# Two recurrences written step by step beside each other, their late inputs in DRAM, the last projection by halves, and a planner that knows matmul tilings

## The chip, the cores and the metric

One NeuronCore of a Trainium2 chip runs one program. Its engines run side by side and wait for each other through semaphores: TensorE (PE; its weight loads are listed as PEld), VectorE (DVE), ScalarE (ACT), GpSimd (POOL) and SyncE (SP), which issues all transfers of this kernel. Matmul operands lie in SBUF, matmul results go to PSUM, weights and spilled tensors lie in DRAM. The metric is device microseconds (us) of one execution, the median of three runs for the kernel before.

## The reference

512 tokens of 1024 columns pass through two blocks. The first has two layers: a gated feed-forward, a mixer (an mLSTM in the first layer, dilated attention in the second, each with cross-attention to 256 memory tokens), another feed-forward. The second block has two layers with a modulated input, and it also carries a context of 256 tokens. Each of its layers joins three mixers: grouped attention, neighbourhood attention, and a recurrence (RWKV-7) of 6 heads that runs over the tokens once forward and once backward:

```python
def _rwkv7_step(S, inp):
    r, w, k, v, kk, b = inp
    sa = jnp.einsum('bhvk,bhk->bhv', S, kk)
    S = S * w[:, :, None, :] - sa[..., None] * b[:, :, None, :] + v[..., None] * k[:, :, None, :]
    return S, jnp.einsum('bhvk,bhk->bhv', S, r)
...
    y_l = jnp.concatenate([yr_l * jax.nn.silu(rg_l), ya_l * jax.nn.silu(ag_l),
                           yn_l * jax.nn.silu(ng_l)], axis=-1) @ w_out
    x = _layer_norm(DEEPNORM_ALPHA * x + gate[:, None] * y_l, ln_g, ln_b)
```

The outputs of both directions are added, normalised by head and gated; then they are projected with the two attentions' outputs, added to x and layer-normalised. The context runs through the same recurrence first, and its final states start those of the tokens. In the second layer the context's outputs are not needed, only its states.

## The kernel before, in words

**Program and order.** The program does not issue instructions. It records operations on named tiles, with `par` weaving parallel branches together. `schedule` then orders the whole list: `simulate` is a list scheduler that runs once from the end (its finishing times become keys of urgency) and once from the start, three rounds. For each engine it takes the most urgent operation that can start, and SBUF and PSUM tiles are slots of a fixed number (`SLOTS`, line 265): 70 slots `t` of 2 KB per partition, 8 PSUM banks `ps`, 14 `S`, one `uv`. `Op._cost` gives durations and `LATENCY` the hops between engines. On TensorE it prefers, within `STAY` (2.0 us of the keys), an operation with the same flag `small` (planned cost under 0.1 us) as the last one. The order of the program's own text decides only among equals.

**Stages.** In order of time: the first layer's feed-forward with the context's input work; the mLSTM; the second feed-forward with the context's first recurrence (`ctx_out(0)`); shared keys and values; the same for the second layer of the first block, whose last feed-forward runs beside `ctx_out(1)`; then for each of the second block's layers `layer_in` (projections), `layer_mix` (attention woven with `rwkv`), `out2` (output projection and layer norm). Large projections are three float32r matmuls for each product (`mm3`), the attention's and the recurrence's products are float32, which the trace shows as two matmul instructions each.

**The recurrence.** Tokens are cut into chunks of 32, four to a block of 128. For one direction `r`, `rwkv_a` makes decays and transformed keys from `k`, `kk`, `r` of `rwkv_in`, and the masks' products `EB`, `EQ`; `rwkv_b` inverts triangular 32x32 systems with 62 small VectorE operations; `rwkv_c` turns the one tile `UV` (values, and under them the right-hand sides) into the recurrence's inputs; `rwkv_d` steps from chunk to chunk. A step has 6 products `pw` (weights from `S`, tiling 64x32), a subtraction on two halves of `UV` (DVE), 6 products `pn` (from `UV`, 64x64), and S = pn + keep (DVE), with keep = S times the decay on POOL. After four steps the block's outputs `y` are 24 products with the old states (64x32) and 12 with `UV` (128x64), written as four of the one and two of the other in turn. `rwkv` runs a, b, c, d for the forward direction and then for the backward one; both use the same `UV`, so the backward `rwkv_c` overwrites what the forward `rwkv_d` reads. The first direction writes `y` by ACT, the second adds to it on DVE. 512 tokens have 16 steps and 4 blocks in each direction, the context's 256 have 8 and 2.

**The last projection.** `out2` works on tokens 256 to 511 and then 0 to 255 (`cuts`). The attention's outputs, the residual and the split operands are loaded or made for all 512 tokens; `rwkv_y`, 192 matmuls of 256 columns, and the layer norm are done by halves. The backward direction, the last one, finishes blocks 3 and 2 first.

Of the kernel before, what the change touches and what calls it, by code (L numbers as in the profile page):

```python
# [16 lines left out]
P = 128  # L17
# [336 lines left out]
class Op:  # L354
    def __init__(self, eng, method, a, k):
        self.eng, self.method, self.a, self.k = eng, method, a, k
        named = [(f"#{i}", x) for i, x in enumerate(a)] + list(k.items())
        refs = [(q in ("#0", "out", "accum_out"), x) for q, x in named if isinstance(x, Ref)]
        self.writes = [x for w, x in refs if w]
        self.reads = [x for w, x in refs if not w]  # L360
        self.cost = self._cost()
        self.small = self.cost < 0.1 and eng == "tensor"

    def _cost(self):
# [3 lines left out]
        if self.eng == "tensor":  # L368
            n = self.writes[0].cols()
            if self.method == "transpose":  # L370
                return 0.84e-3 * n
# [69 lines left out]
def simulate(ops, before, after, key, lag, ahead):  # L441
# [12 lines left out]
    small = False  # L454
# [18 lines left out]
    def best(tight):  # L473
        out = None
        for e in ENGINES:
# [4 lines left out]
            for src, time in ((can[e], lambda x: free[e]), (wait[e], lambda x: x[0])):  # L480
                pick = None
                for x in sorted(src):
# [5 lines left out]
                    if pick and ops[i].small != small:  # L488
                        continue
                    at = room(i, tight)  # L490
                    if at is not None:
                        pick = (max(at, time(x)), key[i], i, e, src, x)
                        if e != "tensor" or src is not can[e] or ops[i].small == small:
                            break
# [6 lines left out]
    while len(order) < n:  # L501
# [6 lines left out]
        if e == "tensor":  # L508
            small = ops[i].small
# [19 lines left out]
def schedule(ops):  # L529
# [11 lines left out]
    lag = lambda i, j: 0.0 if ops[i].eng == ops[j].eng == "tensor" else LATENCY[ops[i].eng]  # L541
# [30 lines left out]
class Prog:  # L572
# [1055 lines left out]
    def rwkv_in(self, l, hp, n, need_y, cut=False):  # L1628
# [22 lines left out]
        d["kk"] = kk  # L1651
        d["v"] = [conv(6 + j) for j in range(3)]
        if need_y:
            d["vd"] = [self.save(v, (P, n)) for v in d["v"]]
            d["r"] = [conv(j) for j in range(3)]

        d["UV"] = self.new("uv", (P, nb, 2, 6, 64))
        for o in (0, 64):
            nc.gpsimd.memset(d["UV"][o:o + 32], 0.0)
        for j in range(3):  # L1660
# [3 lines left out]
            for par in range(2):  # L1664
                for c in range(4):
                    o = 64 * (c % 2 ^ par) + 32
                    self.act(d["UV"][o:o + 32, :, c // 2, 2 * j + par], pv[32 * c:32 * c + 32, :, 64 * par:64 * par + 64])
        return d

    def rwkv_a(self, l, d, r):  # L1670
# [4 lines left out]
        q = dict(D=self.sm((P, n // 32, 3)), KR=[], EB=[], EQ=[], kt=[], be=[])  # L1675
# [11 lines left out]
        if need_y:  # L1687
            first = "kd" not in d
            d.setdefault("kd", []), d.setdefault("pr", [])
        for j in range(3):  # L1690
            ps = self.ps((P, n))
# [12 lines left out]
            q["KR"].append(KR)  # L1704
            for hf in range(nh):
                sl = slice(256 * hf, 256 * hf + 256)
                kap, kc, ec = ch(KR[hf][:, 0]), ch(d["kk"][j][:, sl]), ch(eL[:, sl])
# [6 lines left out]
                if need_y:  # L1714
                    self.mul(KR[hf][:, 1], d["r"][j][:, sl], eL[:, sl])
# [6 lines left out]
            self.mul(bb, bb, d["kk"][j])  # L1722
            self.act(th, th, AF.Identity, scale=L["hka"][:, j:j + 1], bias=L["oka"][:, j:j + 1])
            self.mul(th, th, d["k"][j])
            if need_y and first:
                d["kd"].append(self.save(th, (P, n)))
            elif need_y:
                t = self.load(self.t2((P, n)), d["kd"][j])
                self.tt(t, t, th, ALU.add)
                self.stt(t, d["r"][j], self.c(f"r_k{l}", j), t, ALU.mult, ALU.mult)  # L1730
# [17 lines left out]
            for par in range(2):  # L1748
# [5 lines left out]
                for w, mask, out in [(0, strict, "EB"), (1, incl, "EQ")][:nk]:  # L1754
# [3 lines left out]
                    q[out].append(e.rearrange("p g c t -> p g (c t)"))  # L1758
# [44 lines left out]
    def rwkv_c(self, d, q):  # L1803

        n, nb = d["n"], d["nb"]
        q["zk"] = []
        for j in range(3):
            pb = [self.ps((P, nb, 64)) for _ in range(2)]
            for b in range(nb):
                for par in range(2):  # L1810
                    for a in range(2):
                        self.mm(pb[par][64 * a:64 * a + 64, b], q["EB"][2 * j + par][:, 2 * b + a], d["UV"][:, b, a, 2 * j + par])
# [4 lines left out]
            for par in range(2):  # L1817
# [8 lines left out]
                for c in range(4):  # L1826
                    ro = 64 * (c % 2 ^ par)
                    self.act(d["UV"][ro:ro + 32, :, c // 2, h], pu[32 * c:32 * c + 32, :, par], scale=-1.0)
# [3 lines left out]

    def rwkv_d(self, d, q, r, S):


        n, nb, need_y = d["n"], d["nb"], d["need_y"]
        UV = d["UV"]
        first = "y" not in d
        if first and need_y:
            d["y"] = [self.t2((P, 6, 64)) for _ in range(nb)]  # L1840
        both = [(j, par) for j in range(3) for par in range(2)]
        for step in range(4 * nb):
            g = 4 * nb - 1 - step if r else step
            b, c = g // 4, g % 4
            row = lambda c, par: 64 * (c % 2 ^ par)
            if step % 4 == 0:
                old = {}
                ps = self.ps((P, 2, 3, 64))
                pw, pn = ps[:, 0], ps[:, 1]
            old[c] = S  # L1850
            for j, par in both:
                o, ro = 64 * par, row(c, par)
                self.mm(pw[ro:ro + 32, j], q["zk"][j][o:o + 64, 32 * g:32 * g + 32], S[o:o + 64, j])
            keep = self.new("S", (P, 3, 64))
            self.nc.gpsimd.tensor_tensor(out=keep, in0=S, in1=q["D"][:, g].unsqueeze(2).to_broadcast([P, 3, 64]), op=ALU.mult)
            for par in range(2):
                ro = row(c, par)
                u = UV[ro:ro + 32, b, c // 2, par::2]
                self.tt(u, u, pw[ro:ro + 32], ALU.subtract)
            for j, par in both:  # L1860
                o, ro = 64 * par, row(c, par)
                self.mm(pn[o:o + 64, j], q["be"][j][g // 8][ro:ro + 64, g // 2 % 4, o:o + 64],
                        UV[ro:ro + 64, b, c // 2, 2 * j + par])
            S = self.new("S", (P, 3, 64))
            self.tt(S, pn, keep, ALU.add)
            if not need_y or step % 4 < 3:
                continue
            py = [self.ps((P, 3, 64)) for _ in range(2)]
            for a in range(2):
                for j in range(3):  # L1870
                    for i, par in ((0, 0), (0, 1), (1, 0), (1, 1)):
                        o, cc = 64 * par, 2 * a + (i ^ par)
                        s = P * (b % 2) + 32 * cc
                        self.mm(py[par][32 * cc:32 * cc + 32, j], q["KR"][j][b // 2][o:o + 64, 1, s:s + 32],
                                old[cc][o:o + 64, j], stop=False)
                    for par in range(2):
                        self.mm(py[par][64 * a:64 * a + 64, j], q["EQ"][2 * j + par][:, 2 * b + a], UV[:, b, a, 2 * j + par],
                                start=False)
            for par in range(2):
                y = d["y"][b][:, par::2]  # L1880
                if first:
                    self.act(y, py[par])
                else:
                    self.tt(y, y, py[par], ALU.add)
# [35 lines left out]
    def rwkv(self, l, d, S):  # L1920
        out = []
        for r in range(2):
            q = self.rwkv_a(l, d, r)
            self.rwkv_b(q, r)
            self.rwkv_c(d, q)
            if S is None:
                s0 = self.new("S", (P, 3, 64))
                self.nc.vector.memset(s0, 0.0)
            else:
                s0 = S[r]  # L1930
            out.append(self.rwkv_d(d, q, r, s0))
        return out

    def out2(self, l, d, gates, pa, src, dst, mod, w, n, nxt=None):
# [3 lines left out]
        h, lo = self.parts(n)  # L1938
        for k in range(3, KD):
# [149 lines left out]
```

## Time and profile before

| | |
|---|---|
| median of three runs | 3327.55 us (3325.96 to 3327.77) |
| profiled execution | 3327.22 us, of which the span from first to last instruction is 3325.4 us |
| TensorE | 3217.1 us busy, 21142 matmuls |
| VectorE, ScalarE, GpSimd | 2299.8, 1613.3, 252.0 us busy |
| TensorE clock granted, mean | 0.987 of full speed |
| transfers | 348.41 MB, 105 GB/s |

Busy time of an engine is the union of its instructions' times, and a matmul's end is modelled, so neighbouring matmuls overlap in the profile. What a matmul costs the engine is better read from start to start. All operations are recorded by one helper line, 568, so rows are told apart by tile names and shapes: `ps<-S,t 64*32 64x64` is a matmul into PSUM with weights from an `S` tile, 64 rows by 32 columns of the array, 64 columns streamed.

### The profile page before, as it was taken

Reading aid. Unit: us, or ns where it says so; the run is one execution under the profiler, and the core shown is the slowest. Engines: PE = TensorE matmul, PEld = TensorE weight load, DVE = VectorE, ACT = ScalarE, POOL = GpSimd, SP = SyncE. Lnnn points to the kernel's source line nnn. Section 1 sums busy time; section 2 is a strip of 40 time slices with the busy share of each in tenths; the row PEclk is TensorE's granted clock in tenths of the full one; section 3 lists DMA queues with packets and bytes.
Section 4 is the critical chain, followed back from the end, with each engine's and each line's share of the span. In section 5 each row is a group of like instructions: output and inputs, shape, how many; then the busy total and the mean of one; then the engine's idle time right before and its main releaser. Section 6 shows DMA issues by size and latency. Waiting matters only on the chain. (4 is left out here: it accounts for less than half of the span.)

```text
span 3325.4 us, 55255 instructions
## 1 busy us (share of the span) xinstructions
PE 3217.1 (97%) x21142; PEld 2604.3 (78%) x21142; DVE 2299.8 (69%) x4801; ACT 1613.3 (49%) x3579; POOL 252.0 (8%) x233
## 2 busy tenths in 40 slices
PE   8999999999999999999999999999999898999898
PEld 6788878778877788878886888777877678877677
DVE  9954686575669677677568657587475887575876
ACT  4433464363434344333338535344454974654773
POOL 0000000000000102000001000000120011111111
PEclk9999999999999999999999999999999999999899
DMA  6633332133213334344431422233222232322231
GB/s 227 205 114 124 120 116 80 56 117 101 82 55 101 108 117 143 114 137 154 130 103 38 133 88 89 69 102 120 89 83 93 66 118 94 107 87 85 63 121 43
DMA packets 153489, 348.41 MB, mean 105 GB/s; under 512 B 16644, under 2 KB 60420, under 8 KB 153224
## 3 DMA queue, kind: packets, MB, share of 16 engines
q1 hardware_dynamic: 153224, 344.87, 31.9%
q8 instruction: 166, 2.72, 0.3%
q14 instruction: 99, 0.81, 0.1%
HBM read 315.05 MB, written 29.76 MB: 104 GB/s over the span
## 5 line engine op out<-in xcount | busy, mean ns | idle before, releaser
L568 PE MATMUL ps<-t,t 128*128 128x512 f32 (+6 forms) x15204 | 2865.1, 351 | 63.7 <-DVE t L568 29.6
L568 PEld LDWEIGHTS ps<-t,t 128*128 128x128 f32 (+2 forms) x15204 | 2287.6, 182 | 522.6 <-issue 65.2
L568 ACT ACTIVATE t<-raw 128x512 fp32r<-128x512 f32 (+1 forms) x962 | 565.8, 612 | 762.5 <-PE ps L568 510.5
L568 DVE TENSOR_TENSOR t<-raw,t 128x512 fp32r<-128x512 f32 (+2 forms) x962 | 625.5, 670 | 235.3 <-PE ps L568 169.0
L568 ACT ACTIVATE t<-t 128x512 f32<-128x512 f32 (+8 forms) x739 | 377.7, 525 | 426.4 <-DVE t L568 246.2
L568 DVE TENSOR_TENSOR t<-t,t 128x256 f32<-128x256 f32 (+7 forms) x812 | 417.7, 544 | 91.3 <-ACT t L568 57.1
L568 ACT ACTIVATE t<-ps 128x512 f32<-128x512 f32 (+8 forms) x448 | 216.0, 511 | 219.5 <-PE ps L568 214.6
L568 DVE TENSOR_TENSOR t<-ps,t 128x512 f32<-128x512 f32 (+3 forms) x274 | 178.8, 657 | 185.3 <-PE ps L568 178.2
L568 POOL TENSOR_TENSOR s<-s,const 128x4 f32<-128x4 f32 (+6 forms) x65 | 110.2, 1698 | 1722.4 <-DVE s L568 1714.0
L568 PE MATMUL ps<-const,t 128*128 128x128 f32 (+1 forms) x1116 | 189.0, 291 | 22.5 <-ACT t L568 12.3
L568 DVE SCALAR_TENSOR_TENSOR t<-ps,t 128x512 f32<-128x512 f32 (+3 forms) x229 | 147.5, 648 | 69.2 <-PE ps L568 68.5
L568 PEld LDWEIGHTS ps<-const,t 128*128 128x128 f32 x1116 | 137.4, 149 | 66.1 <-ACT t L568 27.8
L568 PE MATMUL ps<-uv,t 64*64 64x64 f32 (+1 forms) x2208 | 144.1, 230 | 3.2 <-DVE t L568 1.7
L568 PEld LDWEIGHTS ps<-uv,t 64*64 64x64 f32 (+1 forms) x2208 | 103.5, 135 | 52.9 <-issue 14.1
L568 ACT ACTIVATE t<-t,const 128x256 f32<-128x256 f32 (+3 forms) x165 | 102.0, 646 | 52.4 <-DVE t L568 30.5
L568 ACT ACTIVATE uv<-ps 32x128 f32<-32x128 f32 (+1 forms) x288 | 92.5, 322 | 59.4 <-PE ps L568 55.4
L568 DVE SCALAR_TENSOR_TENSOR t<-t,t 128x512 f32<-128x512 f32 (+2 forms) x116 | 76.7, 663 | 64.0 <-ACT t L568 62.6
L568 DVE SCALAR_TENSOR_TENSOR t<-raw,const,t 128x512 f32<-128x512 f32 x168 | 117.9, 744 | 1.4 <-DMA raw<-in_wmod_dram 1.4
L568 DVE TENSOR_TENSOR uv<-uv,ps 32x192 f32<-32x192 f32 x192 | 66.5, 347 | 65.7 <-PE ps L568 58.1
L568 POOL TENSOR_TENSOR S<-S,s 128x192 f32<-128x192 f32 x96 | 62.2, 648 | 599.5 <-DVE S L568 451.0
L568 PE MATMUL ps<-S,t 64*32 64x64 f32 x2112 | 104.0, 224 | 0.6 <-DVE S L568 0.6
L568 ACT ACTIVATE t<-ps,s,s 128x256 f32<-128x256 f32 (+1 forms) x140 | 88.1, 650 | 26.4 <-DVE s L568 26.3
(81 smaller groups left out, 1388.0 us busy)
## 6 DMA issues: line engine op xcount, KB each, us to landing
raw<-in_wgu_dram SPq DMA_DIRECT2D x176, 512.0 KB, 3.6
raw<-in_win_dram SPq DMA_DIRECT2D x88, 512.0 KB, 3.6
raw<-in_wd_dram SPq DMA_DIRECT2D x128, 256.0 KB, 2.7
raw<-in_wmod_dram SPq DMA_DIRECT2D x48, 512.0 KB, 3.8
t<-dram SPq DMA_DIRECT2D x68, 256.0 KB, 2.8
dram<-t SPq DMA_DIRECT2D x68, 256.0 KB, 2.0
t<-dram SPq DMA_DIRECT2D x97, 128.0 KB, 2.2
raw<-in_wd_dram SPq DMA_DIRECT2D x64, 192.0 KB, 2.3
```

The source lines that it names most:

```text
L568: getattr(getattr(tc.nc, op.eng), op.method)(*map(real, op.a), **{q: real(v) for q, v in op.k.items()})
```

## The change

The planner gets the tiling of each TensorE operation (rows and columns of the array that it takes, rounded up to 32, 64 or 128). It prefers the same tiling instead of the same flag `small`, adds 0.12 us to its plan where the tiling changes, adds 0.12 us to a hop into TensorE, and has new costs for matmuls. There are 64 `t` slots instead of 70, two `uv` and 16 `S`.

`rwkv_in` saves `kk`, `k` and `r` to DRAM, and `rwkv_a` loads them for each of three column blocks and each direction. `rwkv_a` also stores the decayed `r` (`rho`) and `EQ` to DRAM, and `rwkv_d` loads them for each block. There is one `UV` for each direction, so `rwkv_a`, `rwkv_b`, `rwkv_c` of both directions come first and one `rwkv_d` steps through both: forward chunk g beside backward chunk 4*nb-1-g. Outputs are written as 24 products with old states for each direction, then 12 with `UV` for each. `out2` loads and splits the attention's outputs and the residual by halves.

```diff
-SLOTS = dict(t=70, raw=4, ps=8, big=3, uv=1, S=14, tmp=2, s8=48, s32=16, s64=4)
+SLOTS = dict(t=64, raw=4, ps=8, big=3, uv=2, S=16, tmp=2, s8=48, s32=16, s64=4)
-LATENCY = dict(tensor=0.2, vector=0.14, scalar=0.15, gpsimd=0.15, sync=3.0)
+LATENCY = dict(tensor=0.22, vector=0.13, scalar=0.15, gpsimd=0.15, sync=3.0)
+INTO_PE = 0.12
+SIDE_BY_SIDE = {(128, 128): 1, (128, 64): 2, (128, 32): 4, (64, 128): 2, (64, 64): 4, (64, 32): 6, (32, 128): 4,
+                (32, 64): 6, (32, 32): 8}
+RETILE = 0.12
...
-            l = self.k["lhsT"]
-            f = 1 / 2.4 if l.base.dt == F32R else 4 / 2.4
-            half = 0.58 if 16 < l.cols() <= 64 else 1.0
-            return 0.002 + 1e-3 * max(n, 64) * f * half
+            if self.k["lhsT"].base.dt == F32R:
+                return 0.0137 + n / 2400
+            one = max(0.003 + n / 1200, 0.11 if self.tiling[1] == P else 0.08)
+            return 2 * max(one / SIDE_BY_SIDE[self.tiling], 0.02)
...
-        if e == "tensor":
-            small = ops[i].small
+        if e == "tensor" and ops[i].tiling != tiling:
+            at, tiling = at + RETILE, ops[i].tiling
...
-        d["kk"] = kk
+        d["kk"] = [self.save(x, (P, n)) for x in kk]
+        d["k"] = [self.save(x, (P, n)) for x in d["k"]]
...
+            q["rho"], q["EQ"] = self.dram((3, P, n)), self.dram((2, 3, P, 2 * nb, 64))
         for j in range(3):
+            xk, xkk = [self.load(self.t2((P, n)), d[x][j]) for x in ("k", "kk")]
+            xr = self.load(self.t2((P, n)), d["r"][j]) if need_y else None
...
         for step in range(4 * nb):
-            g = 4 * nb - 1 - step if r else step
+            gs = (step, 4 * nb - 1 - step)
+            for r, g in enumerate(gs):
...
+                for j, par in both:
+                    o, ro = 64 * par, row(c, par)
+                    self.mm(pw[r][ro:ro + 32, j], qs[r]["zk"][j][o:o + 64, 32 * g:32 * g + 32], S[r][o:o + 64, j])
...
+                rho.append(self.load(self.t2((P, 3, P)), qs[r]["rho"][:, :, P * b:P * b + P].rearrange("j p t -> p j t")))
+                EQ.append([self.load(self.t2((P, 3, 2, 64)), qs[r]["EQ"][par][:, :, 2 * b:2 * b + 2].rearrange("j p g x -> p j g x"))
+                           for par in range(2)])
+            for r, g in enumerate(gs):
+                b = g // 4
+                for a in range(2):
+                    for j in range(3):
+                        for i, par in ((0, 0), (0, 1), (1, 0), (1, 1)):
+                            o, cc = 64 * par, 2 * a + (i ^ par)
+                            self.mm(py[r][par][32 * cc:32 * cc + 32, j], rho[r][o:o + 64, j, 32 * cc:32 * cc + 32],
+                                    old[r][cc][o:o + 64, j], start=(j == 0), stop=False, skip_group_check=True)
+            for r, g in enumerate(gs):
+                b = g // 4
+                for a in range(2):
+                    for j, par in both:
+                        self.mm(py[r][par][64 * a:64 * a + 64, j], EQ[r][par][:, j, a],
+                                d["UV"][r][:, b, a, 2 * j + par], start=False, skip_group_check=True)
...
-            self.rwkv_c(d, q)
...
-            out.append(self.rwkv_d(d, q, r, s0))
+            self.rwkv_c(d, qs[r], r)
...
+        return self.rwkv_d(d, qs, S)
...
-        x = [self.load(self.t2((P, n)), src[m]) for m in range(KD)]
...
         for s in self.cuts(n):
             c = s.stop - s.start
             nt = c // P
+            h, lo = self.parts(c)
+            for k in range(3, KD):
+                self.split(h[k], lo[k], self.load(self.t2((P, c)), pa[k - 3][:, s]))
+            x = [self.load(self.t2((P, c)), src[m][:, s]) for m in range(KD)]
```

## Rows read from the trace of the kernel before

**Rows 1.** The page, part 1: busy us (share of the span) and instructions by engine.
```profile
PE 3217.1 (97%) x21142; PEld 2604.3 (78%) x21142; DVE 2299.8 (69%) x4801; ACT 1613.3 (49%) x3579; POOL 252.0 (8%) x233
```

**Rows 2.** Windows: stretch and length, busy us by engine, granted clock, DMA share, GB/s.
```profile
2320.00:3325.40 1005.40, 939.54 (x8713) 753.58 (x8712) 704.00 (x1638) 580.17 (x1348) 130.09 (x125) 0.97 0.28 88
1300.00:1700.00 400.00, 399.70 (x1817) 327.19 (x1817) 271.60 (x455) 136.57 (x249) 10.81 (x7) 1.00 0.41 131
```

**Rows 3.** Windows of the instructions that touch `S` tiles (PE, PEld, DVE, POOL).
```profile
2500.00:2570.00 70.00, 16.18 (x336) 9.54 (x336) 5.36 (x15) 8.26 (x15) 1.00 0.23 75
2570.00:2700.00 130.00, 4.05 (x56) 1.94 (x56) 0.35 (x1) 0.51 (x1) 0.96 0.29 88
```

**Rows 4.** Waits: engine, who ended them, total us, times, longest us.
```profile
PE ps L568 <- DVE t L568: 44.6, 24, 15.6
PE ps L568 <- ACT t L568: 39.0, 41, 4.0
```

**Rows 5.** Windows inside two of the stalls, columns as in rows 2.
```profile
2615.00:2620.00 5.00, 0.34 (x6) 0.20 (x6) 2.09 (x6) 4.43 (x13) 3.83 (x5) 0.82 0.00 0
2810.00:2815.00 5.00, 1.26 (x6) 0.91 (x4) 3.83 (x12) 4.29 (x12) 2.33 (x1) 0.50 0.14 54
```

**Rows 6.** Timeline of TensorE: start us, us, instruction, count; output products of one block.
```profile
3261.71 0.32 PE L568 MATMUL ps<-S,t 64*32 64x64 f32 x8
3261.96 0.45 PE L568 MATMUL ps<-uv,t 128*64 128x64 f32 x4
3262.33 0.32 PE L568 MATMUL ps<-S,t 64*32 64x64 f32 x8
```

**Rows 7.** The same view of other blocks: shorter turns, and two longer runs.
```profile
2630.17 0.30 PE L568 MATMUL ps<-S,t 64*32 64x64 f32 x4
...
2630.66 0.30 PE L568 MATMUL ps<-S,t 64*32 64x64 f32 x4
...
2529.68 0.54 PE L568 MATMUL ps<-S,t 64*32 64x64 f32 x18
2530.15 1.20 PE L568 MATMUL ps<-t,t 128*128 128x512 f32 x4
```

**Rows 8.** The same view of all engines: one step of the forward recurrence.
```profile
2514.95 0.53 PE L568 MATMUL ps<-S,t 64*32 64x64 f32 x12
2515.41 1.19 PE L568 MATMUL ps<-t,t 128*128 128x512 f32 x4
2515.53 0.71 DVE L568 TENSOR_TENSOR uv<-uv,ps 32x192 f32<-32x192 f32 x2 [1.36 <-PE ps L568]
...
2516.53 0.56 PE L568 MATMUL ps<-uv,t 64*64 64x64 f32 x12
...
2517.24 0.36 DVE L568 TENSOR_TENSOR S<-ps,S 128x192 f32<-128x192 f32 x1 [1.00 <-PE ps L568]
...
2517.92 0.53 PE L568 MATMUL ps<-S,t 64*32 64x64 f32 x12
```

**Rows 9.** The same view: attention's products with values between transposes.
```profile
2634.48 1.09 PE L568 MATMUL ps<-const,t 128*128 128x128 f32 x8
2635.50 0.87 PE L568 MATMUL ps<-t,t 128*64 128x128 f32 x10
2636.30 0.66 PE L568 MATMUL ps<-const,t 128*128 128x128 f32 x4
2636.89 3.36 PE L568 MATMUL ps<-t,t 128*64 128x128 f32 x39
```

**Rows 10.** Groups by shape: count, busy us, mean ns, idle before: products with values.
```profile
L568 PE MATMUL ps<-t,t 128*64 128x128 f32 x1448 | 143.2, 285 | 2.0 <-ACT t L568 1.2 <-ACT uv L568 0.3
```

**Rows 11.** DMA issues: count, KB each, median us from issue to landing.
```profile
t<-dram SPq DMA_DIRECT2D x68, 256.0 KB, 2.8
```

**Rows 12.** Timeline of TensorE near the end, after the last output products.
```profile
3263.57 10.33 PE L568 MATMUL ps<-t,t 128*128 128x256 f32 x84
...
3305.47 0.50 PE L568 MATMUL ps<-const,t 128*128 128x1 f32 x4
```

More of the change, by code (lines that the diff above doesn't have):

```diff
@@ L360, in __init__, with _tiling @@
         self.reads = [x for w, x in refs if not w]
+        self.tiling = self._tiling() if eng == "tensor" else None
         self.cost = self._cost()
-        self.small = self.cost < 0.1 and eng == "tensor"
+    def _tiling(self):
+        l = self.reads[0] if self.method == "transpose" else self.k["lhsT"]
+        up = lambda n: 32 if n <= 32 else 64 if n <= 64 else 128
+        return up(32 * l.v.shape[0]), up(l.cols())
     def _cost(self):
@@ L453, in simulate @@
     can = {e: [] for e in ENGINES}
-    small = False
+    tiling = None
     first, head, done, order = sorted(range(n), key=key.__getitem__), 0, [False] * n, []
@@ L487, in best @@
                         continue
-                    if pick and ops[i].small != small:
+                    same = ops[i].tiling == tiling
+                    if pick and not same:
                         continue
@@ L492, in best @@
                         pick = (max(at, time(x)), key[i], i, e, src, x)
-                        if e != "tensor" or src is not can[e] or ops[i].small == small:
+                        if e != "tensor" or src is not can[e] or same:
                             break
@@ L1654, in rwkv_in @@
             d["vd"] = [self.save(v, (P, n)) for v in d["v"]]
[L1655 to L1659, printed above, removed]
+            d["r"] = [self.save(conv(j), (P, n)) for j in range(3)]
+        d["UV"] = [self.new("uv", (P, nb, 2, 6, 64)) for _ in range(2)]
+        for uv in d["UV"]:
+            for o in (0, 64):
+                nc.gpsimd.memset(uv[o:o + 32], 0.0)
         for j in range(3):
@@ L1714, in rwkv_a @@
                 if need_y:
-                    self.mul(KR[hf][:, 1], d["r"][j][:, sl], eL[:, sl])
+                    self.mul(KR[hf][:, 1], xr[:, sl], eL[:, sl])
+                    nc.sync.dma_start(out=q["rho"][j][:, sl], in_=KR[hf][:, 1])
             ps = self.ps((P, n))
@@ L1831, in rwkv_c, with rwkv_d @@
             q["zk"].append(zk)
-    def rwkv_d(self, d, q, r, S):
+    def rwkv_d(self, d, qs, S):
         n, nb, need_y = d["n"], d["nb"], d["need_y"]
[L1837 to L1840, printed above, removed]
+        if need_y:
+            d["y"] = [None] * nb
         both = [(j, par) for j in range(3) for par in range(2)]
+        row = lambda c, par: 64 * (c % 2 ^ par)
+        S = list(S)
+        old, pw, pn = [{}, {}], [None] * 2, [None] * 2
@@ L1842, in rwkv_d @@
         for step in range(4 * nb):
-            g = 4 * nb - 1 - step if r else step
[L1844 to L1863, printed above, removed]
@@ L1866, in rwkv_d @@
+            for r in range(2):
+                S[r] = self.new("S", (P, 3, 64))
+                self.tt(S[r], pn[r], keep[r], ALU.add)
             if not need_y or step % 4 < 3:
                 continue
[L1868 to L1878, printed above, removed]
```

119 lines of the change are left out of this document (75 added, 44 removed).

## The prediction

> **What bounds the kernel now.** The page's first part comes first: TensorE is busy 97% of the span, VectorE 69%, ScalarE 49% [rows 1]. The windows say what that is worth. From 1300 to 1700 us the feed-forward keeps TensorE busy 399.7 of 400 us at full clock with 1817 matmuls, 0.22 us each, and weight loads busy 327 us, 82% [rows 2]. Over the whole span loads are busy 78%, so against that dense stretch about 4% of 3325 us, 142 us, are not dense. The last thousand us, the second block's token layers, hold most of it: loads at 75%, 65.9 us without a matmul, mean clock 0.97 [rows 2].
>
> The Trainium skill (Perfetto Trace Analysis, section Identifying the Most-Contended Engine) says that matmul busy time flatters TensorE and that the share of weight loads is the better measure of distance from the roof. By its 78% there would be 22%, some 720 us, to win; the dense stretch of this trace reads only 82% with no gap to fill, so the trace puts it at 142 us and I go by that.
>
> The loss has two forms. One is open waits: TensorE waits 44.6 us for VectorE and 39.0 us for ScalarE [rows 4], and a wait drags the clock down with it: in 2810 to 2815 it is busy 1.26 of 5 us at half clock, 1.2 GHz [rows 5]. The other hides inside busy time: each change from one tiling of the array to another. In the outputs of a block 8 matmuls from `S` and 4 from `UV` alternate at 0.62 us a turn (3261.71 to 3262.33) [rows 6], although 18 `S` matmuls in a row take 0.47 us until the next start, 26 ns each [rows 7]; at 26 ns the 8 need 0.21 of their 0.25 us, and the 4 take 0.37 us. The change touches both forms and hardly any arithmetic, so the question is how much of the 142 us it can reach.
>
> **A, output products regrouped: -30 us.** There are 20 blocks times directions with outputs: 2 x 4 in each of two layers, 2 x 2 in the context's first layer. Each has 24 products with old states and 12 with `UV`, 48 and 24 matmul instructions. Now they come in turns of 8 and 4, six turns of 0.62 us = 3.7 us [rows 6], or in turns of 4 and 2, twelve of 0.49 us (2630.17 to 2630.66) = 5.9 us [rows 7]. Grouped, the 48 cost 48 x 26 ns = 1.25 us [rows 7], and the 24 cost 24 x 55 ns = 1.3 us (0.37 us for 4, less a change of 0.15). That is 2.55 us and saves 1.2 to 3.3 us a block. I take 1.5, nearer to rows 6, whose pattern is that of the program: 20 x 1.5 = 30 us. TensorE is the busy engine at all these places. Bounds 0 (all of it returns as waiting) and 66.
>
> **B, steps of both directions together: -10 us.** A step makes two excursions into small tilings between large matmuls [rows 8]. The `pw` burst takes 0.46 us (2514.95 to 2515.41) for 12 matmuls that at 26 ns need 0.31; the rest, 0.15 us, plus the delay in front of it, is about 0.2 us per excursion. 96 single steps become 48 double ones; if both directions' bursts merge, 96 excursions go, 19 us. But the new program order only decides among equals: the planner may start the forward recurrence early, since it no longer waits for the other direction's half of anything. Bounds 0 and 19; I take half.
>
> The Trainium skill (TensorEngine Tiling (Array Packing), section Tiling Modes) says that different tiles load and multiply in parallel. It would make merged bursts cheaper still; the rows for it are in the first rival.
>
> **C, the planner sees tilings elsewhere: -10 us.** Attention's products with values (128x64) and the transposes (128x128) counted as the same kind before. Eight transposes between them take 1.02 us from start to start and four take 0.59 [rows 9]; the difference is 0.11 us a transpose, so a round trip itself costs 0.59 - 0.43 = 0.16 us, 0.2 with the delay in front. 1448 such matmuls [rows 10] in runs of 10 to 39 [rows 9] are 37 to 145 round trips, 7 to 29 us. Preferring the same tiling may also put off an urgent operation by up to the 2 us that `STAY` allows. Bounds -29 and +10.
>
> **D, fewer open waits in the token layers: -18 us.** With one `UV`, the backward direction's last preparation waits for the forward recurrence's end. The rows of `S` show it: 336 matmuls from 2500 to 2570, then 130 us with 56, and only then the second recurrence [rows 3]. In that gap VectorE and ScalarE carry the backward preparation and attention's softmax together, and TensorE starves (0.34 of 5 us from 2615, ScalarE 4.43) [rows 5]. With two `UV` and `kk`, `k`, `r`, `EQ`, `rho` in DRAM the planner may spread that preparation. Slots allow it: for layer one the projection's operands take 32 (weights) + 16 + 8 + 16 = 72 slots `t`, above the 70 there were; by halves they take 32 + 8 + 4 + 16 = 60 of 64, and the nine `t` of `kk`, `k` and `r` no longer live through `rwkv`. Of the 65.9 us [rows 2] about 20 come after the last projection (3305.47) [rows 12] and stay. Of the other 46 a third, 15 us, goes, and 3 us with the half clock that follows such waits. What is late next is ScalarE in the same stretches, since none of its work goes away. Bounds: -46, and a loss that the third rival prices.
>
> **E, both halves finish together: +3 us.** The backward direction, run last, finished blocks 3 and 2 first, so half the projection was under way while it ended: after the last output products 41.9 us pass to the last matmul of the projection (3263.57 to 3305.47) [rows 12], where 2 x 192 matmuls at 0.12 us (84 in 10.33 us) [rows 12] need 47. Now block 3 gets its forward part and block 0 its backward part in the last step. 5 us more remain, and the heads' norm, a chain of small operations on three engines, stands open in front; the products with the attentions' parts cover it as long as PSUM's 8 banks allow. Against it the first half's layer norm now lies under the second half's matmuls, where TensorE idled before (2810) [rows 5]. Bounds -10 and +20.
>
> **F, transfers: 0.** Per token layer: 9 saves, 2 copies of `UV`, 12 stores of `rho`, 12 of `EQ`, 18 loads in `rwkv_a`, 24 in `rwkv_d`, 13 more in `out2`, together 90; the context adds some 60 and 20. That is 260 on SP's queue and some 42 MB on 348. DMA engines are at 0.28 in the last stretch and 0.41 in the dense one [rows 2], so there is room, and the 2.8 us of a load [rows 11] lie inside the 25 us by which the planner lets SP run ahead. Uncovered, a load, and a store taken as long, stand once before each of eight preparations (two directions of two token layers and two context layers), 45 us. The second `UV`'s memset is on POOL, busy 8% [rows 1].
>
> **The sum.** -30 - 10 - 10 - 18 + 3 = -65 us. The profiled execution took 3327.22 us (span 3325.4 and 1.8 around it), 0.3 below the median, so 3262 us.
>
> **Rivals.** First, everything merges: A at 45, B at 19, C at 15, D at 30. The two directions' bursts then cover four positions of the array instead of two, since chunks g and 4*nb-1-g differ in parity. Eight `S` matmuls on four positions take 0.25 us until the next start [rows 6], twelve on two take 0.46 us [rows 8]; less 0.1 for the change of tiling that is 19 and 30 ns each, so 24 merged ones save 0.26 us, 96 times 25 us if the planner interleaves them. Part of that: about -120, 3207 us. For it speaks that all of it is TensorE time; against it that list order interleaves only by chance.
>
> Second, it doesn't do what it says: the planner runs the directions apart whatever the text says. B is nothing and D half: -30 - 10 - 9 + 3, 3281 us. For it: the forward direction is ready first, and nothing holds it.
>
> Third, slower: the recurrence runs bare at the end of each layer. A step takes 2.97 us now (2514.95 to 2517.92) [rows 8], and TensorE fills all but 0.96 us of it with large matmuls. A double step adds the other direction's 0.71 and 0.36 us on VectorE, 4.0 us, of which TensorE has own work for 1.7. If attention is used up by then, 2.3 us stand idle in each of 32 double steps, 74 us, and at 1.2 GHz [rows 5] the bursts cost some 25 us more. Against savings of A and C, 40 us, that is +59 at most and a loss from 18 bare double steps on; typically 3350 us. For it: both directions now end at the same time, last. Against it: double steps need 32 x 4.0 = 128 us with large matmuls for 74 where the single ones needed 64 x 2.0 = 128, and attention fills the 130 us between the recurrences now [rows 3].
>
> Fourth, no change: the saved TensorE time returns as waiting for ScalarE and VectorE in the token layers, and the new order loses elsewhere what it wins: 3322 us. For it: the waits by ScalarE and VectorE already end most idle time [rows 4]. Against it: busy shares of 70% and 58% there [rows 2].
>
> **How the numbers follow.** The forecast has 0.43, the second rival 0.14, the first 0.20, the third 0.12, the fourth 0.11. About 0.2% (7 us) is what a measurement of this kernel can tell. Faster: 0.43 + 0.14 + 0.20 and a little of the fourth, 0.78; same 0.09; slower 0.13. Terms A to E at their own bounds make the forecast's own range 3225 to 3300. The first rival's better half and the third's worse half are left out: 3205 to 3335.
>
> **What would show it.** A: in the timeline after each fourth step, long runs of 64x32 and then of 128x64 instead of turns of 8 and 4. B: bursts of 24 instead of 12; single ones speak for the second rival. C: fewer and longer runs of products with values. D: no gap of 130 us between recurrences, fewer us of waits for ScalarE and VectorE, the last stretch's clock above 0.97. E: more than 41.9 us from the last outputs to the last projection. The prediction is wrong if TensorE's busy time falls by less than 40 us, or if it falls and idle time grows by as much.

## The result and the profile after

| | before | after |
|---|---|---|
| median of four runs, us | 3327.66 (3325.96 to 3328.76) | 3243.43 (3238.34 to 3245.64) |
| ratio, 95% interval | | 0.9745 (0.9728 to 0.9762) |
| span of the profiled execution, us | 3325.4 | 3242.6 |
| changes of tiling | 1392 | 866 |

The changed kernel is 84 us faster, 2.5%; the forecast was 65 us faster. "Changes of tiling" counts the places in TensorE's timeline where two neighbouring matmuls have different rows or columns of the array.

The page of the kernel after, part 1, answers rows 1:
```profile
PE 3127.8 (96%) x21142; PEld 2581.6 (80%) x21142; DVE 2308.9 (71%) x4807; ACT 1610.8 (50%) x3589; POOL 269.8 (8%) x245
```
The number of matmuls is the same and they take 89.3 us less of busy time; the span shrank by 82.8. The whole gain is TensorE's busy time, and idle time grew from 108.3 to 114.8 us.

Windows of about equal work in both kernels, cut where the first load of the shared keys' weights and the decay weights of each token layer are issued; columns as in rows 2. Before:
```profile
0.00:1219.00 1219.00, 1190.61 (x6703) 972.59 (x6704) 836.30 (x1687) 536.65 (x1155) 54.77 (x61) 1.00 0.35 115
1219.00:2332.00 1113.00, 1098.91 (x5795) 887.48 (x5793) 769.52 (x1494) 505.15 (x1090) 67.61 (x48) 0.99 0.34 109
2332.00:2843.00 511.00, 482.81 (x4488) 390.88 (x4487) 362.52 (x843) 301.61 (x702) 72.71 (x66) 0.97 0.28 92
2843.00:3325.40 482.40, 444.73 (x4163) 353.33 (x4161) 331.47 (x778) 269.87 (x634) 56.87 (x58) 0.96 0.26 82
```
and after:
```profile
0.00:1190.00 1190.00, 1164.59 (x6706) 964.20 (x6707) 836.68 (x1684) 536.02 (x1156) 62.85 (x69) 1.00 0.40 125
1190.00:2310.00 1120.00, 1103.51 (x5929) 901.69 (x5929) 779.39 (x1515) 508.55 (x1102) 74.19 (x50) 0.99 0.36 112
2310.00:2786.00 476.00, 447.52 (x4363) 373.68 (x4363) 358.92 (x829) 296.07 (x695) 76.08 (x69) 0.96 0.43 133
2786.00:3242.60 456.60, 412.16 (x4149) 342.00 (x4147) 333.91 (x782) 270.20 (x638) 56.64 (x58) 0.95 0.40 124
```
The first stretch, which holds the context's first recurrence, is 29 us shorter, the two token layers 35 and 26 us; the second stretch, whose recurrence has no outputs, is 7 us longer. Part of the last two differences is work that moved across a cut: after, the second stretch holds 134 matmuls more (58 of them 128x512) and the third 125 fewer (64 of them 128x512). At the groups' mean times that is about 17 us, an estimate, so with equal work the second stretch would be some 10 us shorter and the third some 18. In the last one not-busy time went from 37.7 us (482.4 less 444.7) to 44.4.

The groups of matmuls that answer rows 10, with those of the recurrence, after (x count, busy us, mean ns, idle before):
```profile
L583 PE MATMUL ps<-t,t 128*64 128x128 f32 x1448 | 126.6, 285 | 5.7 <-DVE t L583 4.6 <-ACT t L583 0.8
...
L583 PE MATMUL ps<-S,t 64*32 64x64 f32 x2112 | 68.0, 222 | 0.8 <-DVE t L583 0.8
L583 PE MATMUL ps<-uv,t 128*64 128x64 f32 x1056 | 61.5, 231 | 1.4 <-DVE uv L583 0.9 <-issue 0.5
L583 PE MATMUL ps<-uv,t 64*64 64x64 f32 x1152 | 57.2, 230 | 3.6 <-DVE uv L583 3.5
```
The last three groups were these before:
```profile
L568 PE MATMUL ps<-S,t 64*32 64x64 f32 x2112 | 104.0, 224 | 0.6 <-DVE S L568 0.6
L568 PE MATMUL ps<-uv,t 128*64 128x64 f32 x1056 | 90.2, 233 | 2.8 <-DVE t L568 1.7 <-DVE uv L568 1.1
L568 PE MATMUL ps<-uv,t 64*64 64x64 f32 x1152 | 55.5, 226 | 0.3 <-ACT t L568 0.2
```
By the profile's modelled ends each of these small matmuls still takes its 220 to 230 ns; what fell is how long the group holds the engine, because more of them lie on top of each other. In the timeline of TensorE after, output products come as rows 6 never had them, 48 in 1.08 us and 16 in 0.87 us:
```profile
3100.27 1.15 PE L583 MATMUL ps<-S,t 64*32 64x64 f32 x48
3101.35 0.44 PE L583 MATMUL ps<-const,t 128*128 128x128 f32 x2
...
3103.14 0.94 PE L583 MATMUL ps<-uv,t 128*64 128x64 f32 x16
3104.01 0.53 PE L583 MATMUL ps<-S,t 64*32 64x64 f32 x12
```
Both recurrences now run at once: 720 matmuls from `S` in one stretch of 130 us, where rows 3 had 336, a gap, and the rest (columns as there):
```profile
2570.00:2700.00 130.00, 27.80 (x720) 19.24 (x720) 10.46 (x30) 16.89 (x30) 0.97 0.44 136
```
Yet open waits are no smaller. The waits of TensorE after, which answer rows 4, sum to 104.7 us in that view against 98.2 before, and the mean granted clock went from 0.987 to 0.982. It was VectorE's part that grew; ScalarE's shrank:
```profile
PE ps L583 <- DVE t L583: 53.5, 28, 13.4
PE ps L583 <- ACT t L583: 36.5, 39, 3.6
```

### The profile page after: what moved, and what is told of

Same layout as the page of the kernel before. It is cut to its first block, busy times and chain, and to the rows that moved or that the text cites. A ratio compares the mean times of both kernels' runs of the same rounds, so it can differ in the third digit from the quotient of the medians.

```text
span 3242.6 us, 55887 instructions
## 1 busy us (share of the span) xinstructions
PE 3127.8 (96%) x21142; PEld 2581.6 (80%) x21142; DVE 2308.9 (71%) x4807; ACT 1610.8 (50%) x3589; POOL 269.8 (8%) x245
## 2 busy tenths in 40 slices
DMA packets 205383, 394.47 MB, mean 122 GB/s; under 512 B 20789, under 2 KB 105397, under 8 KB 204985
## 4 chain that ended last, share of the span: by engine, by line
PE 80%; DVE 10%; ACT 5%; DMA 2%; issue 2%; POOL 1%; SPq 0%; ACTq 0%; POOLq 0%; DVEq 0%
PE ps L583 80%; DVE t L583 7%; ACT t L583 4%; ACT big L583 1%; DVE s L583 1%; DVE big L583 1%; ACT uv L583 1%; DVE tmp L583 1%; POOL s L583 1%; DMA t<-dram 1%; DMA raw<-in_wgu_dram 0%; DMA raw<-in_wmod_dram 0%; DMA dram<-t 0%; POOL uv L583 0%; DMA raw<-in_wout_dram 0%
## 5 line engine op out<-in xcount | busy, mean ns | idle before, releaser
L583 PE MATMUL ps<-t,t 128*128 128x512 f32 (+6 forms) x15204 | 2809.6, 351 | 44.6 <-DVE t L583 27.8
L583 ACT ACTIVATE t<-raw 128x512 fp32r<-128x512 f32 (+2 forms) x962 | 565.5, 612 | 776.2 <-PE ps L583 496.0
L583 DVE TENSOR_TENSOR t<-raw,t 128x512 fp32r<-128x512 f32 (+2 forms) x962 | 632.8, 674 | 310.0 <-PE ps L583 167.0
L583 ACT ACTIVATE t<-t 128x512 f32<-128x512 f32 (+10 forms) x749 | 378.0, 521 | 400.1 <-DVE t L583 204.0
L583 ACT ACTIVATE t<-ps 128x512 f32<-128x512 f32 (+5 forms) x448 | 215.8, 512 | 212.1 <-PE ps L583 203.7
L583 PE MATMUL ps<-const,t 128*128 128x128 f32 (+1 forms) x1116 | 195.6, 295 | 38.6 <-ACT t L583 22.1
L583 PE MATMUL ps<-uv,t 64*64 64x64 f32 (+1 forms) x2208 | 116.7, 230 | 5.0 <-DVE uv L583 4.4
L583 PEld LDWEIGHTS ps<-uv,t 64*64 64x64 f32 (+1 forms) x2208 | 93.2, 138 | 34.4 <-issue 15.2
L583 POOL TENSOR_TENSOR t<-t,s 64x512 f32<-64x512 f32 x36 | 52.1, 1459 | 481.0 <-DVE t L583 351.4
L583 DVE TENSOR_TENSOR big<-big,tmp 128x31 f32<-128x31 f32 (+15 forms) x248 | 84.6, 341 | 4.6
```

Of the source, the lines that this page charges most:

```text
L583: getattr(getattr(tc.nc, op.eng), op.method)(*map(real, op.a), **{q: real(v) for q, v in op.k.items()})
```

## Experiments

Theory "tilings": the gain is TensorE time that changes between array tilings had cost. Rival "release": it comes from freeing the second recurrence from the first (two `UV`, late inputs in DRAM). Ratios are to the kernel before.

**The planner alone**, in the program of before:
```diff
-        self.small = self.cost < 0.1 and eng == "tensor"
+        self.tiling = self._tiling() if eng == "tensor" else None
...
+            at, tiling = at + RETILE, ops[i].tiling
```


> The program of before (one UV, recurrences one after the other, outputs in turns, projection whole, 70 slots t) with the new planner: tilings, costs and hops. Theory 'tilings': TensorE pays 0.1 to 0.12 us for each change of tiling, and the planner saves some by itself, those of attention above all, while the turns of the output products stay, since matmuls into one PSUM bank keep their order in the plan: 3327 less 15 to 35, 3300 us. Rival 'release': the gain came from freeing the backward preparation (two UV, late inputs), so the planner alone gives 3320 to 3330 us.

3303.39 us, 0.9929 (0.9914 to 0.9944), 1189 changes of tiling.

**The program alone**, with the planner of before:
```diff
-SIDE_BY_SIDE = {(128, 128): 1, (128, 64): 2, (128, 32): 4, (64, 128): 2, (64, 64): 4, (64, 32): 6, (32, 128): 4,
...
-RETILE = 0.12
...
+        self.small = self.cost < 0.1 and eng == "tensor"
```


> The new program (two UV, both directions step by step, outputs regrouped, late inputs in DRAM, projection by halves, 64 slots t) with the old planner. Theory 'tilings': the regrouped outputs alone save about 45 us of TensorE time and the double steps little, 3275 to 3290 us, with open waits as before (about 100 us). Rival 'release': nearly the whole gain, 3240 to 3260 us, with open waits clearly below 98 us. Third reading, program and planner need each other: both parts alone give under 15 us, 3312 us or more here.

3271.86 us, 0.9836 (0.9822 to 0.9851), 1105 changes. The two parts add: 23 + 55 = 78 of 84 us. The groups separate them. With the planner alone, products with values (first line) fall from rows 10 and those from `S` and `UV` stay:
```profile
L583 PE MATMUL ps<-t,t 128*64 128x128 f32 x1448 | 128.5, 288 | 1.4 <-DVE t L583 1.0
L583 PE MATMUL ps<-S,t 64*32 64x64 f32 x2112 | 103.5, 227 | 1.8 <-DVE S L583 1.6
```
With the program alone it is the other way round:
```profile
L568 PE MATMUL ps<-t,t 128*64 128x128 f32 x1448 | 148.5, 290 | 3.1 <-ACT t L568 3.0
L568 PE MATMUL ps<-S,t 64*32 64x64 f32 x2112 | 72.8, 221 | 0.2 <-DVE t L568 0.2
```
Its waits sum to 95.7 us. That it lands between the two expected ranges of "tilings" and "release" in time is settled by this: the time went out of matmul groups, not out of waits.

**Tiling kept, costs and hops of before:**
```diff
-LATENCY = dict(tensor=0.22, vector=0.13, scalar=0.15, gpsimd=0.15, sync=3.0)
-INTO_PE = 0.12
+LATENCY = dict(tensor=0.2, vector=0.14, scalar=0.15, gpsimd=0.15, sync=3.0)
+INTO_PE = 0.0
...
```


> The changed kernel with the old matmul costs and hops in the planner, but the preference for the same tiling and the 0.12 us for a change kept. Theory 'tilings': the preference is what counts in the planner, 3243 to 3262 us. Rival 'truer plan': what counts is that durations and hops into TensorE fit the chip, so this loses what the planner had won, 3275 to 3290 us.

3240.01 us, 0.9741 (0.9725 to 0.9757), 871 changes: the changed kernel's time. The kernel with the program alone has the same costs and hops and took 3271.86 us, so the preference for the same tiling, with its 0.12 us for a change, is worth 32 us in the new program.

**Costs and hops kept, the old flag for small matmuls:**
```diff
-                    same = ops[i].tiling == tiling
+                    same = ops[i].kind == tiling
...
-            at, tiling = at + RETILE, ops[i].tiling
+            tiling = ops[i].kind
```


> The changed kernel with the new matmul costs and hops, but the old flag for small matmuls in place of the tiling, and nothing added for a change. Theory 'tilings': attention's products with values and the recurrence's bursts are interrupted again, 3270 to 3290 us, and TensorE's busy time is 25 to 45 us above the changed kernel's 3127.8. Rival 'truer plan': 3243 to 3255 us.

3306.53 us, 0.9935 (0.9920 to 0.9950), 1145 changes, worse than the theory had it. Products with values hold 156.2 us, waits sum to 107.6. Next to the program with the whole old planner (3271.86 us) the new costs and hops alone made the plan 35 us worse; why is not settled. So of the planner's edits the preference for the same tiling and the 0.12 us planned for a change are what pays; the two were not tried apart.

**Outputs in turns again:**
```diff
+                        for par in range(2):
+                            self.mm(py[r][par][64 * a:64 * a + 64, j], EQ[r][par][:, j, a],
+                                    d["UV"][r][:, b, a, 2 * j + par], start=False)
```


> The changed kernel with the output products written in turns again, four with old states and two with UV. Theory 'tilings': matmuls into one PSUM bank keep their order in the plan, so the turns come back whatever the planner prefers and cost what regrouping saved, 35 to 45 us: 3275 to 3290 us, nearly all of it in TensorE's busy time of the S and UV products. Rival 'the planner does it': with four banks open at once it can line up equal tilings across directions, 3243 to 3258 us.

3265.63 us, 0.9822 (0.9806 to 0.9839), 1046 changes. It falls between the ranges: the turns cost 22 us, about half of what regrouping was thought to save. The groups of `S` and `UV` lie between 68.0 and 61.5 after and 104.0 and 90.2 before:
```profile
L583 PE MATMUL ps<-S,t 64*32 64x64 f32 x2112 | 85.7, 224 | 0.6 <-DVE S L583 0.6
L583 PE MATMUL ps<-uv,t 128*64 128x64 f32 x1056 | 82.6, 231 | 2.3 <-DVE t L583 1.0 <-DVE uv L583 0.8 <-ACT t L583 0.5
```
The planner's dependences keep the order in each bank; that with four banks open it lines up some equal tilings across them would explain the half that stayed, but was not looked at by itself.

**Two `UV`, the text by directions:**
```diff
-        return self.rwkv_d(d, qs, S)
+            S = self.rwkv_d(d, qs, S, (r,))
...
```


> The changed kernel with two UV, but the text runs the forward direction to its end (preparation and steps) before the backward one; outputs stay regrouped in each direction. Theory 'the planner sets the order': nothing but equals changes, 3238 to 3250 us, and double steps appear or not as the keys have it. Rival 'side by side': merged bursts and shared output groups are lost, one change of tiling in each of some 190 places, 3258 to 3268 us.

3289.27 us, 0.9893 (0.9878 to 0.9908), 956 changes: 46 us of the 84 are gone, more than the rival said. The recurrences are apart again, in windows of the `S` instructions:
```profile
2480.00:2550.00 70.00, 10.28 (x288) 7.45 (x288) 5.70 (x16) 9.37 (x15) 1.00 0.38 120
2550.00:2660.00 110.00, 2.02 (x96) 1.54 (x96) 0.00 (x0) 0.84 (x1) 0.91 0.35 109
2660.00:2745.00 85.00, 13.35 (x384) 9.88 (x384) 5.33 (x15) 9.88 (x15) 0.91 0.39 121
```
Part of the loss is TensorE's clock. In the trace of this kernel matmuls take 118 us at a granted clock of 0.50 (1.2 GHz), in that of the changed one 85 us. Where two 128x512 matmuls follow each other without a wait, the second starts after 427 ns at that level and after 227 ns at full clock, so about half of such time is lost, and the difference is worth some 17 of the 46 us, an estimate. All runs of the one kernel show a mean clock of 0.978 to 0.981, all of the other 0.982 to 0.984.

**One `UV`, the text by directions:**
```diff
-        d["UV"] = [self.new("uv", (P, nb, 2, 6, 64)) for _ in range(2)]
+        d["UV"] = [self.new("uv", (P, nb, 2, 6, 64))] * 2
...
```


> As the kernel with the text apart, but with one UV for both directions again, so that the backward rwkv_c waits for the forward outputs. Theory 'tilings': open waits are not where the gain is, 3240 to 3258 us. Rival 'release': with TensorE's work shorter the serial chain now ends layers, open waits grow by 20 to 40 us over the changed kernel's 105, 3265 to 3285 us.

3292.06 us, 0.9902 (0.9887 to 0.9917), to be read against the 3289.27 with two `UV`: the intervals overlap. With the text by directions the second `UV` is worth nothing that shows; what it is good for is that both recurrences can run at the same time.

**Text by directions, outputs in tiles of their own:**
```diff
+                    self.act(d["y"][r][b][:, par::2], py[r][par])
...
+                self.tt(d["y"][0][b], d["y"][0][b], d["y"][1][b], ALU.add)
```


> As the kernel with two UV and the text apart (3289 us), but each direction writes its own output tiles, which are added at the end; nothing makes the backward direction wait for the forward one any more. Theory 'order of the additions': what kept the recurrences apart there is that the backward outputs of block 3, its first, are added to the forward outputs of block 3, its last; without it both run at the same time and most of the 46 us come back, 3245 to 3262 us. Rival 'text': the planner's first pass takes its urgency from the text, so the recurrences stay apart, 3280 to 3295 us.

3268.62 us, 0.9830 (0.9814 to 0.9846), between the ranges. 21 of the 46 us come back, but not for the expected reason: no matmul run of one recurrence joins the other's.
```profile
2480.00:2550.00 70.00, 13.25 (x372) 9.38 (x372) 5.69 (x16) 8.82 (x15) 1.00 0.32 99
2550.00:2660.00 110.00, 0.72 (x12) 0.39 (x12) 0.00 (x0) 0.51 (x1) 0.92 0.37 114
2660.00:2745.00 85.00, 11.48 (x372) 8.40 (x372) 5.62 (x16) 8.48 (x15) 1.00 0.39 120
```
So the additions were not what kept the recurrences apart. The text, from which the planner's first pass takes its urgency, is what is left; that room for tiles has no part in it was not tried. The other 25 us go with running apart.

**k, kk and r kept in SBUF:**
```diff
-        d["k"] = [self.save(x, (P, n)) for x in d["k"]]
...
-            xk, xkk = [self.load(self.t2((P, n)), d[x][j]) for x in ("k", "kk")]
+            xk, xkk = d["k"][j], d["kk"][j]
...
```


> The changed kernel with k, kk and r kept in SBUF (no saves and loads of them; rho and EQ still go through DRAM), with 64 slots. Theory: nine slots more held through both preparations leave the planner less room for attention, 3250 to 3275 us. Rival: room is not what binds, and the 30 loads and 24 saves fewer change nothing, 3238 to 3250 us.

3265.43 us, 0.9824 (0.9809 to 0.9838): 22 us slower than the change, with waits of 117.4 us against 104.7. The expectation miscounted the transfers: 66 loads and 33 saves fewer are issued, 374.39 MB in place of 394.47. Fewer transfers and a slower kernel speak for room in SBUF, which is what the edit takes away.

**The projection by halves alone**, in the kernel before:
```diff
+            x = [self.load(self.t2((P, c)), src[m][:, s]) for m in range(KD)]
...
```


> The kernel before with the last projection's operands loaded and split by halves, and nothing else. Theory: room in SBUF does not bind there and half-width splits cost ScalarE and VectorE 3 us, 3320 to 3332 us. Rival 'room': the projection's operands, 72 slots whole and 60 by halves, held up attention and the next layer's input, so open waits fall, 3295 to 3315 us.

3328.59 us, 1.0001 (0.9991 to 1.0010): nothing, as the theory said.

**Directions interleaved product by product:**
```diff
-                for j, par in both:
+            for j, par in both:
+                for r, g in enumerate(gs):
...
```


> The changed kernel with the two directions' products taken in turn, one by one, inside each burst (pw, pn, outputs), so that neighbours lie on other positions of the array; the last 24 products with UV alternate between the two column halves. Theory 'positions': neighbours on four positions cost 19 ns where two cost 30, and products with UV on two halves cost half of the 55 ns that one half costs; the S, UV and 64x64 groups, 166 us from start to start in the changed kernel, fall by 25 to 40 us: 3205 to 3225 us. Rival 'the planner breaks it up': its keys already mix the directions, or set them apart, and the text changes nothing: 3235 to 3250 us.

3224.80 us, 0.9701 (0.9684 to 0.9719), faster than the change. The time is in the range of "positions", its reason only in part: from start to start, waits left out, the three groups fall from 165.7 to 156.1 us, 10 instead of 25 or more. The rest of the 19 us is a plan with fewer waits (97.1 us, 7.6 fewer) and the clock: 0.985 to 0.988 in its runs, with 55 us of matmul time at half clock in place of 85, worth some 15 us by the same estimate. Waits and clock alone are more than 19 us, so what the three groups won was lost again in others, and it is not shown that interleaving makes TensorE's own work shorter.

**Fewer changes still:** the interleaved kernel with a longer reach for the same tiling.
```diff
-STAY = 2.0
+STAY = 4.0
```


> The kernel with the two directions interleaved (3224.8 us) with STAY at 4 us instead of 2: the planner may pass over more urgent matmuls for one of the same tiling within 4 us of urgency. Theory 'tilings': fewer changes at about 0.12 us each, some 150 fewer, 3203 to 3215 us, with TensorE's busy time down by 10 to 20 us. Rival 'urgency': what is put off stands on the chain through ScalarE and VectorE, so open waits grow by what the changes save or more, 3222 to 3245 us.

3221.95 us, 0.9682 (0.9669 to 0.9695), 723 changes against 903, and no clear gain on the interleaved kernel: the intervals overlap. TensorE's busy time falls by 14 us more (3113.3 to 3099.1) and comes back as waiting. The largest waits of the interleaved kernel:
```profile
PE ps L583 <- DVE t L583: 46.8, 26, 13.0
PE ps L583 <- ACT t L583: 39.4, 50, 3.0
```
and of this one:
```profile
PE ps L583 <- DVE t L583: 59.3, 39, 13.1
PE ps L583 <- ACT t L583: 39.5, 40, 6.2
PE ps L583 <- ACT big L583: 4.3, 1, 4.3
```
All waits sum to 115.4 us against 97.1. The rival had it right that waiting takes back what the changes save; that what is put off is what ScalarE and VectorE wait for would explain it and was not traced. These two are the fastest versions.

## Why the prediction was right or wrong

The direction and the main mechanism were right: the gain is TensorE's busy time around changes of tiling. All fourteen kernels, set against their counts of changes, lie about a line of 0.155 us a change (526 changes fewer are 82 us), with deviations of up to 31 us. So the count goes with the size and does not give each plan's time. Part of the deviations goes with the clock: the two kernels with the text by directions and shared output tiles lie 25 us above the line, at mean clocks of 0.979 and 0.981, and the interleaved kernel lies 31 below it, at 0.987.

**A, output products: right, mis-sized.** Forecast 30 us, between bounds of 0 and 66. From each matmul's start to the next, waits of over 0.15 us left out, the groups of `S` and `UV` (128x64) took 85.6 + 75.1 us before and take 60.2 + 54.9: 45.6 us, the `pw` bursts included. The 48 products cost 1.08 us where I had 1.25; those with `UV` cost 54 ns each (16 in 0.87 us), as forecast. I put the saving near the longer turns of rows 6, while the trace of before has 42 runs of 8 `S` matmuls and 102 of 4, as in rows 7. But this is where the time was lost and not what regrouping alone is worth: with the text by directions the two groups still take only 65.5 + 54.7 us, 40 of the 46 us less than before, and that kernel is just 14 us faster than the planner alone (3289.27 against 3303.39 us).

**B, double steps: wrong in how, though side by side counts.** Runs of 64x64 products from `UV` number 100 before and 102 after; of these 11 have 24 matmuls, 51 the 12 of a single step, and most others are pieces of a step, as in the timeline of the kernel after, where two bursts of 12 stay apart:
```profile
3106.59 0.56 PE L583 MATMUL ps<-uv,t 64*64 64x64 f32 x12
3107.08 0.50 PE L583 MATMUL ps<-t,t 128*128 128x256 f32 x2
3107.51 0.56 PE L583 MATMUL ps<-uv,t 64*64 64x64 f32 x12
```
So they are not there in this half of the step: that group went from 48.8 to 50.6 us from start to start. The `pw` bursts carry the same names as the output products, so their share of the 10 us cannot be read apart. But I held that the text "only decides among equals", as the description of the kernel before does too; that was wrong twice: matmuls into one PSUM bank keep the text's order, and the text sets the first pass's urgency. Writing the directions apart costs 46 us, some 17 of them by the clock, and 25 us with outputs of their own. What side by side gains is spread over the large matmuls too (the 128x512 group from start to start: 2142.3 us after, 2159.7 with the text apart); which of it is changes of tiling and which the plan is not settled.

**C, attention: right, a little small.** 10 us forecast; products with values go from 128.8 to 112.9 us from start to start, with the planner alone to 116.4, and from 198 runs to 154.

**D, open waits: this step failed.** "Of the other 46 a third, 15 us, goes, and 3 us with the half clock": waits grew from 98.2 to 104.7 us, and the clock fell: matmuls take 62 us at half clock before and 85 after, which costs some 11 us by the estimate above instead of giving 3 back. After 2320 us TensorE is without a matmul for 72.7 us where rows 2 had 65.9:
```profile
2320.00:3242.60 922.60, 849.94 (x8463) 707.75 (x8461) 688.80 (x1603) 561.01 (x1323) 122.81 (x124) 0.95 0.41 128
```
With the text by directions, one `UV` or two makes no difference (3292.06 and 3289.27 us). VectorE and ScalarE have about the same work in a shorter stretch, 75% and 61% busy there instead of 70% and 58% [rows 2]. What I said would be late next, ScalarE, was not: over the whole span waits that ScalarE ends fell from 46.0 to 41.6 us in that view, and those that VectorE ends grew from 47.1 to 59.1. Why VectorE's work comes late more often is not settled. That room in SBUF matters was right as a fact and wrong as a gain: with `k`, `kk` and `r` kept in SBUF the waits are 117 us and not 105.

**E, the joint finish: right in sign.** From the last output products on, 48.9 us pass to the last matmul of the projection where rows 12 had 41.9; the timeline after:
```profile
3171.58 2.03 PE L583 MATMUL ps<-uv,t 128*64 128x64 f32 x36 [0.91 <-DVE uv L583]
3173.54 1.45 PE L583 MATMUL ps<-t,t 128*128 128x256 f32 x10
...
3222.40 0.50 PE L583 MATMUL ps<-const,t 128*128 128x1 f32 x4
```
(3173.54 to 3222.40). That is 7 us where I had 5. The cover that I set against it, the first half's layer norm under the second half's matmuls, does not show: in the last window time without a matmul grew from 37.7 to 44.4 us.

**F, transfers: right.** 46 MB more (394.47 against 348.41, forecast 42), and no transfer among the reasons for which TensorE waits in that view.

**What the five terms left out:** the large matmuls between the excursions. The 128x512 group fell by 22.9 us from start to start (2165.2 to 2142.3) with nothing changed in it. In part that is the delay that each excursion puts on the large matmul in front of it: at full clock 250 of the 9120 stand before another tiling in the trace of before and 130 after, and take about 0.1 us longer there than the others (342 against 234 ns before), some 14 us; the rest is not attributed. Measured so, A 46, C 16 and this 23 are about the whole of the 84 us, and the other groups and the waits cancel. That is a balance of where time left, not of what each edit is worth.

Of the rivals, the second (planned apart) does not hold, since the recurrences run together, and the third (bare steps) does not show: large matmuls lie between the bursts. The fourth (it all returns as waiting) does not hold either: of 89.3 us of busy time 6.5 came back as idle time. Of what the first gave to interleaving, 25 us, the interleaved kernel shows 10 in the three groups. That the sum came within 19 us is in part luck: A, C and the large matmuls took some 45 us more than forecast, while D and B missed by more than 30 the other way. And the forecast's own range of 3225 to 3300 us does not follow from the terms: their bounds add up to 3157 to 3357, D's loss left out.

## What to carry to other kernels

An engine that reads 97% busy can still hold time: look for short matmuls of different tilings in turn, take their price from start to start, and group them by tiling, in the text too where a planner must keep the order within a bank. A freed dependence need not shorten the bounding engine's waits: here they went from 98.2 to 104.7 us, and from ScalarE to VectorE. Before you give a difference between two plans to an edit, look at how much of it is the granted clock. After each such step ask again which engine the waits name: here a further 180 changes fewer won 14 us of TensorE time and returned 18 us of waiting.

## What the runs showed of the hardware

A change of array tiling costs TensorE about 0.1 us inside what the profile calls busy: with no wait, a 128x512 matmul is followed by the next after 227 ns, and by a first 64x32 one after 327 (medians over the trace of before). At a granted clock of 0.50 the 227 ns are 427. `S` products on several positions of the array start every 22 ns (48 in 1.08 us) where twelve on two positions take 30 ns each (0.46 us in rows 8, less 0.1 for the change). And with the two directions taken in turn, the three small groups fell only from 165.7 to 156.1 us, so the 25 to 40 us that were expected of further positions were not reached; whether the planner's order or the array limits it was not tried.
